# A hybrid encoder block: input projections and retention output by seven products for eight, with the token blocks kept in SBUF and the retention run head by head

## The chip, the cores and the metric

The kernel runs on one core of one Trainium2 chip. The time is the device time of one execution in microseconds (us); the three runs shown are summed up by their median. A core has TensorE (PE, with its weight loads PEld), VectorE (DVE), ScalarE (ACT), GpSimd (POOL) and a queue that issues the transfers (SP).

## The reference, cut to what matters

D_MODEL is 1024, the sequence 1024 tokens with 16 meta tokens ahead of it, all in float32. One projection of 5792 columns feeds two token mixers and their gates:

```python
def _mixer(u, w_in, ...):
    proj = u @ w_in
    rq, rk, rv, rg, a_cq, a_ckv, a_kr, a_gret, a_gmla = jnp.split(proj, SPLIT_IDX, axis=-1)
    rq = _apply_rope(rq ...); rk = _apply_rope(rk ...) * (RET_DK ** -0.5)      # 8 heads of 64
    y_ret = _head_group_norm(_bidir_retention(rq, rk, rv, decay_f, decay_b), gn_w)   # dv 128
    y_ret = (jax.nn.silu(rg) * y_ret) @ w_ret_out
    c_q, c_kv = _rmsnorm(a_cq, q_norm_w), _rmsnorm(a_ckv, kv_norm_w)           # ranks 384, 256
    ...                                                                        # MLA attention, 8 heads
    merged = jax.nn.sigmoid(a_gret) * y_ret + jax.nn.sigmoid(a_gmla) * y_mla
    return merged @ w_o
```

u is the RMS norm of x. The retention works in chunks of 128 tokens: inside a chunk scores times a decay mask, between chunks a state that is carried forward and one backward. After the mixer come a residual sum, a SwiGLU FFN with its own norm, and a final norm.

## The kernel before

A float32 product is made of three matmuls in the chip's fp32r type (`mm3`, L122 to L124): each operand is split into a high part (an ACT cast) and a low part (a DVE subtraction), and high by high, high by low and low by high are summed in PSUM.

*Input projections.* u is held transposed as eight pairs of tiles `uh`/`ul` of 128 by 1040. `weights()` (L112 to L118) loads 128 output columns and splits them; `gemm` walks eight k tiles, so each 512 columns of result take 24 matmuls. v is made the other way round, tokens as the output rows, with 256-column products; pair 0's v is made while x comes in (L236 to L238).

*Retention.* Four pairs of heads. For each pair v, the rotated q and k and two gates (rg, through Silu) are projected and stay in SBUF; then `core(p, ...)` runs both heads: k transposed and weighted (`kw`), chunk sums u (L376), a scan of 14 DVE steps (L379, L382), and for each half of four chunks scores (L388), the mask (L390), y (L394, L395), the group norm (L400 to L406), a transposition (L409) and the product with Silu (L411), whose result z goes to DRAM (`z_d`). A scheduler orders each engine's instructions by what is ready and by the order of the program, so projections of the next work stand between the pieces of a head.

*After it.* Six sigmoid gates of the attention branch go to `s_d`. z comes back in eight tiles, split by ACT (L456) and POOL (L457); then for each of eight column tiles a gate product (L437, L438) and the product with w_ret_out, whose sum is multiplied by the gate (L467) into `r_d`. Then the latents ckv and cq (L490, L491), their norms, the shared rotary key, the rotary queries, the last two gates, and the attention. The FFN already uses `seven`: of a product of 2 by 2 blocks (256 output columns, 512-token halves) it makes seven block products "11", "t2", "t3", "n1", "21", "t4", "22" from sums and differences of blocks, where eight would do without sums. They share four PSUM banks; POOL makes the weight sums, ACT and DVE split them (L925, L926), and DVE puts the four results together.

## Time and profile before

| what | value |
|---|---|
| median of three runs | 1809.23 us (1808.49 to 1812.77) |
| the profiled execution | 1811.09 us, its span 1809.3 us, granted TensorE clock 0.994 |
| busy in the span | PE 1776.5 us, DVE 1117.9, ACT 788.1, POOL 628.5 |
| matmuls of the plain input projections and retention output | L122 to L124: 496 + 128 of 512 columns each, and narrower ones |
| first matmul, first score of the attention | 4.95 us, 736.8 us |

Busy is the time in which an engine executed something. A row of windows reads: from:to, its length, then for PE, PEld, DVE, ACT and POOL the busy time with the count of instructions begun in it, the granted clock, the DMA share and GB/s. A group's row has line, engine, operation, output<-inputs, shape, count, then busy us and mean ns of one, then idle time before it and what ended it. A row of the timeline has start and duration in us, and in brackets the idle time before it.

### The profile page before, as it was taken

The numbers are of one execution on the slowest core, as the hardware profiler recorded it, in microseconds if no ns is written. First come the engines' busy times: TensorE is split into PE (matmuls) and PEld (weight loads), VectorE is DVE, ScalarE is ACT, GpSimd is POOL, SyncE is SP. The second block draws the span as 40 slices with busy tenths as digits, with TensorE's granted clock in tenths as the row PEclk, the third lists the DMA queues.
The fourth block names the chain that finished last, engine by engine and source line by source line (L and its number), as shares of the span: only waits on it lengthen the run. The fifth ranks groups of instructions, "written<-read, shape, count | busy, mean of one in ns | idle before, by whom it ended". The sixth has DMA issues, their size and how long they took to land.

```text
span 1809.3 us, 25989 instructions
## 1 busy us (share of the span) xinstructions
PE 1776.5 (98%) x9434; PEld 1525.2 (84%) x9434; DVE 1117.9 (62%) x2124; ACT 788.1 (44%) x1461; POOL 628.5 (35%) x523
## 2 busy tenths in 40 slices
PE   8999999999999999999999999999999999999997
PEld 8898989888788898899989888788888888777787
DVE  6655454544222253787879666876666666877866
ACT  6724242433211133677778445533333333544434
POOL 5303030301200012143242432676667666533422
PEclk9999999999999999999999999999999999999999
DMA  6011111114312212210112555333332333754512
GB/s 218 36 47 49 46 54 41 53 70 146 117 70 71 78 43 85 69 47 28 38 49 71 178 171 174 100 105 107 107 119 88 105 105 105 235 198 150 153 51 93
DMA packets 92495, 175.02 MB, mean 97 GB/s; under 512 B 12032, under 2 KB 26944, under 8 KB 92368
## 3 DMA queue, kind: packets, MB, share of 16 engines
q1 hardware_dynamic: 92368, 173.38, 28.9%
q8 instruction: 74, 1.21, 0.3%
q14 instruction: 53, 0.43, 0.1%
HBM read 129.58 MB, written 43.69 MB: 96 GB/s over the span
## 4 chain that ended last, share of the span: by engine, by line
PE 85%; DVE 6%; ACT 3%; DMA 2%; issue 2%; POOL 1%; SPq 0%; DVEq 0%; POOLq 0%; ACTq 0%
PE mm L934 28%; PE mm L122 13%; PE mm L123 13%; PE mm L124 13%; PE o L693 3%; PE t L663 2%; DVE slot L139 1%; PE s L122 1%; PE s L123 1%; PE s L124 1%; DMA slot<-f_d 1%; PE tr L388 1%; PE y L395 1%; PE u L376 1%; PE y L394 1%
## 5 line engine op out<-in xcount | busy, mean ns | idle before, releaser
L934 PE MATMUL mm<-slot,slot 128*128 128x512 f32 x2604 | 595.6, 390 | 8.4 <-DVE slot L926 3.8
L934 PEld LDWEIGHTS mm<-slot,slot 128*128 128x128 f32 x2604 | 489.1, 188 | 113.8 <-DVE slot L926 5.8
L925 ACT CAST slot<-slot 128x512 fp32r<-128x512 f32 (+1 forms) x238 | 138.7, 583 | 292.5 <-PE mm L934 285.4
L122 PE MATMUL mm<-uh,wh 128*128 128x512 f32 (+2 forms) x640 | 242.6, 379 | 1.0 <-DVE rk L331 0.6
L123 PE MATMUL mm<-ul,wh 128*128 128x512 f32 (+2 forms) x640 | 243.5, 380 | 0.0
L124 PE MATMUL mm<-uh,wl 128*128 128x512 f32 (+2 forms) x640 | 242.3, 379 | 0.0
L926 DVE TENSOR_TENSOR slot<-slot,slot 128x512 fp32r<-128x512 f32 (+1 forms) x238 | 200.5, 843 | 34.4 <-ACT slot L925 34.1
L122 PEld LDWEIGHTS mm<-uh,wh 128*128 128x128 f32 x640 | 120.3, 188 | 23.7 <-DVE rk L331 1.0
L124 PEld LDWEIGHTS mm<-uh,wl 128*128 128x128 f32 x640 | 120.5, 188 | 21.0
L123 PEld LDWEIGHTS mm<-ul,wh 128*128 128x128 f32 x640 | 120.1, 188 | 20.8
L117 ACT CAST wh<-wr 128x1024 fp32r<-128x1024 f32 x51 | 53.2, 1049 | 152.5 <-PE mm L123 120.6
L139 DVE TENSOR_TENSOR slot<-slot,slot 128x512 fp32r<-128x512 f32 x123 | 102.4, 847 | 15.2 <-ACT slot L138 14.9
L653 DVE TENSOR_SCALAR_CACHE_REDUCE pr<-s,sq_c 128x384 f32<-128x384 f32 (+1 forms) x192 | 103.2, 573 | 7.7 <-PE t L671 5.6
L138 ACT CAST slot<-slot 128x512 fp32r<-128x512 f32 x123 | 74.6, 620 | 71.3 <-DMA slot<-f_d 29.4
L124 PE MATMUL mm<-slot,slot 128*128 128x512 f32 (+1 forms) x288 | 105.4, 366 | 0.0
L123 PE MATMUL mm<-slot,slot 128*128 128x512 f32 (+1 forms) x288 | 105.3, 366 | 0.0
L122 PE MATMUL mm<-slot,slot 128*128 128x512 f32 (+1 forms) x288 | 105.2, 367 | 0.0
L666 DVE TENSOR_TENSOR ptl<-t,pth 128x512 fp32r<-128x512 f32 x128 | 85.7, 684 | 19.6 <-ACT pth L665 18.9
L665 ACT CAST pth<-t 128x512 fp32r<-128x512 f32 x128 | 71.9, 580 | 26.0 <-PE t L663 25.6
L910 POOL TENSOR_TENSOR slot<-slot,slot 128x512 f32<-128x512 f32 (+1 forms) x34 | 50.2, 1478 | 90.1 <-DVE slot L926 31.1
L118 DVE TENSOR_TENSOR wl<-wr,wh 128x1024 fp32r<-128x1024 f32 x51 | 67.5, 1326 | 19.1 <-ACT wh L117 17.4
L913 POOL TENSOR_TENSOR slot<-slot,slot 128x512 f32<-128x512 f32 (+1 forms) x34 | 43.2, 1272 | 103.4 <-DVE slot L926 99.9
(349 smaller groups left out, 3582.7 us busy)
## 6 DMA issues: line engine op xcount, KB each, us to landing
wr<-in_w_in SPq DMA_DIRECT2D x37, 512.0 KB
f_d<-slot SPq DMA_DIRECT2D x71, 256.0 KB
slot<-f_d SPq DMA_DIRECT2D x71, 256.0 KB
slot<-in_w_g SPq DMA_DIRECT2D x44, 256.0 KB
slot<-in_w_u SPq DMA_DIRECT2D x44, 256.0 KB
slot<-in_w_dq SPq DMA_DIRECT2D x48, 192.0 KB
slot<-in_w_o SPq DMA_DIRECT2D x32, 256.0 KB
z_d<-ay SPq DMA_DIRECT2D x16, 256.0 KB
```

The source lines that it names most:

```text
L118: dve.tensor_sub(lo, raw, f(hi))
L122: pe.matmul(ps, sh, mh, start=start, stop=False)
L123: pe.matmul(ps, sh, ml, start=False, stop=False)
L124: pe.matmul(ps, sl, mh, start=False, stop=stop)
L138: act.copy(hi, t)
L139: dve.tensor_sub(lo, t, f(hi))
L653: dve.tensor_scalar(pr[:, c], ps[:, :n], sq_c[:, qb : qb + 1], None, ALU.mult, ALU.max, accum_out=mx[:, j : j + 1])
L665: act.copy(pt[0][d], tp)
L666: dve.tensor_sub(pt[1][d], tp, f(pt[0])[d])
L925: act.copy(hi, side[b])
L926: dve.tensor_sub(low, side[b], f(hi))
L934: pe.matmul(ps, sw[:, ks], sx, start=begins and q == qs[0] and i == 0, stop=q == nq - 1 and i == 2, skip_group_check=True)
```

## The change

All input projections (23 groups of 256 columns, `win(0)` to `win(22)`, in the order rg, v, q, k, both gates, ckv, cq with kr) and the retention output (4 groups) use `seven`, which moves ahead of them and takes its pools as an argument. The 14 tiles by 4 of u's blocks (`U`, high and low of seven block forms) stay in SBUF until the latents are made; the same buffers then take z's blocks (`Z`). The 16 meta tokens have narrow matmuls of their own (L214). Results that were used at once now go to DRAM and come back: rg, v (transposed on TensorE first), q, k and both sets of gates.

```diff
+    def seven(pools, srcs, blocks, meta=None):
+        wr, ws, wh_, wl_, pm_ = pools
...
+        pool.tensor_add(s1, a21, a22)
+        pool.tensor_sub(s2, s1, a11)
+        pool.tensor_sub(a21, a11, a21)
+        side = {"11": a11, "t2": s2, "t3": a21, "n1": s1, "21": a12, "t4": a22, "22": s2}
...
+        def prod(b, qs=range(nq)):
...
+                if b == "22":
+                    pool.tensor_sub(s2, s2, a12)
...
+                act.copy(hi, side[b])
+                dve.tensor_sub(low, side[b], f(hi))
...
+                for i, (sw, sx) in enumerate(((wh, xh), (wh, xl), (wl, xh))):
+                    pe.matmul(ps, sw[:, ks], sx, start=begins and q == qs[0] and i == 0,
+                              stop=q == nq - 1 and i == 2, skip_group_check=True)
...
+    def seven_out(prod, pl, post, rest=None):
...
+        act.copy(e, prod("11", r[0]))
+        dve.tensor_add(e, prod("t2", r[1]), e)
...
-        pm = sb(c1, "ps_mm", 3, space=PSUM)
-        pc = sb(c1, "ps_core", 1, space=PSUM)
-        pt2 = sb(c1, "ps_turn", 2, space=PSUM)
+        bt1 = sb(c1, "tokens", 4)
+        wr1, ws1 = sb(c1, "w1r", 5), sb(c1, "w1s", 2)
+        wh1, wl1 = sb(c1, "w1h", 3), sb(c1, "w1l", 3)
+        cr = sb(c1, "c1", 6)
+        pm = sb(c1, "ps_mm", 5, space=PSUM)
+        pc = sb(c1, "ps_core", 3, space=PSUM)
...
+        def bsplit(nm, t):
+            hi, lo = mk(bt1, (P, 512), "h" + nm, F32R), mk(bt1, (P, 512), "l" + nm, F32R)
+            act.copy(hi, t)
+            dve.tensor_sub(lo, t, f(hi))
+            return hi, lo
...
+                U[q]["11"] = bscale("11", x11, w1)
+                act.mul(g12, x12, w1)
+                dve.scalar_tensor_tensor(n1, x11, w1, g12, ALU.mult, ALU.subtract)
+                act.mul(g22, x22, w2)
+                pool.tensor_add(t2, g22, n1)
+                U[q]["t2"] = bsplit("t2", t2)
...
+        cw = sb(cc, "core", 1)
+        ay = sb(cc, "ay", 6)
...
+        def z_sums(p):
+            n1, t3, t2, t4 = [slot(ay) for _ in range(4)]
+            for t, i in ((n1, 0), (t3, 7), (t2, 6), (t4, 4)):
+                load(t, z_d[p, i])
+            pool.tensor_sub(n1, n1, t3)
+            pool.tensor_sub(t3, t2, t3)
+            pool.tensor_add(t2, t2, n1)
+            pool.tensor_sub(t4, t4, t2)
+            for t, i in ((n1, 3), (t3, 2), (t2, 1), (t4, 5)):
+                store(z_d[p, i], t)
...
+        fillers = [(2, rg_post(2)), (3, rg_post(3))]
+        fillers += [(12 + i, gate_post(g_d if i < 4 else s_d, 2 * (i % 4))) for i in range(8)]
...
+        for p in range(4):
+            t = core_pair(p)
+            for h in range(2):
+                core(p, h, *t)
+                filler()
+            z_sums(p)
+        while fillers:
+            filler()
+        cc.close()
...
+        Z = [{} for _ in range(4)]
+        for i, nm in enumerate(NAMES):
+            for q in range(4):
+                raw = slot(cr)
+                load(raw, z_d[q, i])
+                Z[q][nm] = bsplit(nm, raw)
...
+        for j in range(4):
+            seven_out(seven(w7, A["w_ro"][j], Z), cr, ret_post(j))
```

Line numbers after: in `seven` the weight sums are L183 to L185 and L199, the weight split L201 and L202, the matmul L209, those of the meta tokens L214 (48 rows by 128); `seven_out` puts the quarters together in L225 to L234. Splits of blocks are L260 and L261; with the norm's weight L267, in the sums of the first part L308 and L325. `core`'s tiles q, k, v, `qw` and `st`, some of them in two buffers before, have one each. Its chunk sums are L535, scores L552, the mask L554, y L558 and L559, the norm L564 to L570, the transposition L573 and z L574; the sums of z are L581 to L587. The latents are L626 and L627, their squares' sums L634, z's loads L709, the rotary queries L717 to L746, the product with the gate L753. Where the code says that a filler follows each head, the scheduler may take its matmuls earlier, as each engine is free.

How the engines' rows stand at three places. First DVE at the program's start. Before, `ul` is a tile of u's low part, `wl` one of v's weights:

```order
L229 SCALAR_TENSOR_TENSOR ul_26_118<-xk_69_173,cols_74,uh_18_110 128x256
L231 TENSOR_TENSOR wl_164<-wr_162,wh_163 128x256
L229 SCALAR_TENSOR_TENSOR ul_26_118<-xk_69_173,cols_74,uh_18_110 128x272
L229 SCALAR_TENSOR_TENSOR ul_26_118<-xk_69_173,cols_74,uh_18_110 128x512
L229 SCALAR_TENSOR_TENSOR ul_27_119<-xk_70_174,cols_74,uh_19_111 128x1040
L231 TENSOR_TENSOR wl_164<-wr_162,wh_163 128x256
L229 SCALAR_TENSOR_TENSOR ul_28_120<-xk_71_175,cols_74,uh_20_112 128x1040
L231 TENSOR_TENSOR wl_164<-wr_162,wh_163 128x256
L229 SCALAR_TENSOR_TENSOR ul_29_121<-xk_72_176,cols_74,uh_21_113 128x1040
```

After, `l`, `lt`, `ln` are low parts of blocks "11", "t2" or "t3", and "n1"; slots are weights or sums of blocks:

```order
L267 SCALAR_TENSOR_TENSOR l_47_174<-slot_137,cols_74,h_46_173 128x512
L202 TENSOR_TENSOR slot_196<-slot_139,slot_195 128x512
L308 SCALAR_TENSOR_TENSOR slot_170<-slot_137,cols_74,slot_169 128x512
L202 TENSOR_TENSOR slot_212<-slot_148,slot_211 128x512
L202 TENSOR_TENSOR slot_204<-slot_156,slot_203 128x512
L261 TENSOR_TENSOR l_141_451<-slot_171,h_140_450 128x512
L261 TENSOR_TENSOR ln_53_191<-slot_170,hn_52_190 128x512
L267 SCALAR_TENSOR_TENSOR l_83_261<-slot_250,cols_74,h_82_260 128x512
L202 TENSOR_TENSOR slot_228<-slot_140,slot_227 128x512
L308 SCALAR_TENSOR_TENSOR slot_257<-slot_250,cols_74,slot_256 128x512
L261 TENSOR_TENSOR lt_49_182<-slot_172,ht_48_181 128x512
L267 SCALAR_TENSOR_TENSOR l_98_313<-slot_302,cols_74,h_97_312 128x512
```

Where two kinds alternated, block differences, block splits and weight splits now stand in one row, a 512-column piece each; they reach to row 62.

Second, TensorE at the end of the retention. Before, `mm` is a gate of the attention branch and `tr_3601` the last transposition of the last head:

```order
L122 MATMUL mm_3968<-uh_22_114,wh_3935 128x512
L123 MATMUL mm_3968<-ul_30_122,wh_3935 128x512
L124 MATMUL mm_3968<-uh_22_114,wl_3936 128x512
L122 MATMUL mm_3968<-uh_23_115,wh_3935 128x512
L409 MATMUL tr_3601<-ident_63,ay_3596 128x128
L123 MATMUL mm_3968<-ul_31_123,wh_3935 128x512
L409 MATMUL tr_3601<-ident_63,ay_3596 128x128 x2
L124 MATMUL mm_3968<-uh_23_115,wl_3936 128x512
L409 MATMUL tr_3601<-ident_63,ay_3596 128x128
L122 MATMUL mm_3968<-uh_24_116,wh_3935 128x512
L123 MATMUL mm_3968<-ul_32_124,wh_3935 128x512
L124 MATMUL mm_3968<-uh_24_116,wl_3936 128x512
```

After, `mm_4658` is y and `mm_4685` the transposition of head 7's second half, `mm_5391` the sums of the key norm, and `mm_5424` the second half of group 21 (the query latent):

```order
L559 MATMUL mm_4658<-st_4573,qw_4570 128x128
L558 MATMUL mm_4658<-v_4566,slot_4656 128x128
L559 MATMUL mm_4658<-st_4573,qw_4570 128x128
L573 MATMUL mm_4685<-ident_63,slot_4680 128x128
L677 MATMUL mm_5380<-ident_63,slot_5377 128x16
L573 MATMUL mm_4685<-ident_63,slot_4680 128x128 x3
L677 MATMUL mm_5380<-ident_63,slot_5377 128x16
L152 MATMUL mm_5391<-ones_68,lss_5188 128x1 x8
L152 MATMUL mm_5391<-ones_68,lss_5188 16x1
L209 MATMUL mm_5424<-h_124_414,slot_5499 128x512
L209 MATMUL mm_5424<-l_125_415,slot_5499 128x512
L209 MATMUL mm_5424<-h_124_414,slot_5500 128x512
```

The products that stood among the pieces of the last head now stand ahead of it and behind it; from row 2236 to 2285 there is no L209. POOL at that place, after, where `lss` holds the squares for the key norm and L582 to L585 are the sums of pair 3:

```order
L547 TENSOR_TENSOR slot_4647<-slot_4647,rstd_b_125 128x512
L634 TENSOR_TENSOR lss_5188<-lss_5188,slot_5374 128x512
L582 TENSOR_TENSOR slot_4844<-slot_4844,slot_4845 128x512
L583 TENSOR_TENSOR slot_4845<-slot_4846,slot_4845 128x512
L584 TENSOR_TENSOR slot_4846<-slot_4846,slot_4844 128x512
L585 TENSOR_TENSOR slot_4847<-slot_4847,slot_4846 128x512
L634 TENSOR_TENSOR lss_5188<-lss_5188,slot_5351 128x512
L634 TENSOR_TENSOR lss_5188<-lss_5188,slot_5388 128x16
L199 TENSOR_TENSOR slot_5574<-slot_5574,slot_5568 128x512
```

The squares' last sums, which L152 needs, have come to stand behind the sums of z.

Third, the retention output. Before, TensorE's first product with z (`zh`) stands between gate products:

```order
L122 MATMUL mm_4068<-uh_25_117,wh_4058 128x512
L123 MATMUL mm_4068<-ul_33_125,wh_4058 128x512
L124 MATMUL mm_4068<-uh_25_117,wl_4059 128x512
L122 MATMUL mm_4096<-zh_537_4010,wh_4064 128x512
L122 MATMUL mm_4123<-uh_18_110,wh_4058 128x512
L123 MATMUL mm_4123<-ul_26_118,wh_4058 128x512
L124 MATMUL mm_4123<-uh_18_110,wl_4059 128x512
L122 MATMUL mm_4123<-uh_19_111,wh_4058 128x512
```

After, DVE's row ahead of the weights of block "21" of the first output group (`slot_6189`); `l_1231` and `l_1234` are the last two of 28 subtractions that split z, `mm_6013` to `mm_6067` the rotary queries:

```order
L261 TENSOR_TENSOR l_1231_5960<-slot_5957,h_1230_5959 128x512
L261 TENSOR_TENSOR l_1234_5966<-slot_5963,h_1233_5965 128x512
L739 TENSOR_TENSOR slot_6033<-mm_6013,slot_6009 128x512
L740 TENSOR_TENSOR slot_6034<-mm_6023,slot_6010 128x512
L739 TENSOR_TENSOR slot_6043<-mm_6023,slot_6009 128x512
L740 TENSOR_TENSOR slot_6044<-mm_6013,slot_6010 128x512
L744 TENSOR_TENSOR slot_6033<-slot_6033,slot_6038 128x512
L744 TENSOR_TENSOR slot_6043<-slot_6043,slot_6048 128x512
L739 TENSOR_TENSOR slot_6077<-mm_6057,slot_6053 128x512
L740 TENSOR_TENSOR slot_6078<-mm_6067,slot_6054 128x512
L202 TENSOR_TENSOR slot_6189<-slot_6100,slot_6188 128x512
L739 TENSOR_TENSOR slot_6087<-mm_6067,slot_6053 128x512
```

The split of z moved from POOL to DVE, and the weights of the fifth product stand behind all of it and behind the rotary queries' first part; TensorE's row has 48 matmuls of that group ahead of this product.

More of the change, by code (lines that the diff above doesn't have):

```diff
@@ L19 @@
 NS, NT, NO = 3, 3, 2
-G2 = 6
 D = 1024
@@ L166, in build, with half @@
+    def half(name):
+        return slice(0, 512) if name[1] == "1" else slice(512, 1024)
     right, right2 = ExitStack(), ExitStack()
@@ new lines, in squares, with input_norm @@
+                    pool.tensor_add(ss[c], ss[c], t)
+        def input_norm():
+            t = slot(xl)[:, : KT * NM]
+            load(t, A["xm"])
+            act.square(t, t)
+            dve.tensor_reduce(ssm, t.rearrange("p (k t) -> p t k", t=NM), axis=AX.X, op=ALU.add)
+            ps = mk(pc, (P, 512), "mm")
+            for b in range(NB):
+                pe.matmul(ps[:, b : b + 1], ss[b // 4][:, (b % 4) * P : (b % 4) * P + P], ones, start=True, stop=True)
+            pe.matmul(ps[:NM, NB : NB + 1], ssm, ones, start=True, stop=True)
@@ new lines, in z_sums, with gate_post, post @@
+        def z_sums(p):
[8 more added lines that the diff above has]
+                store(z_d[p, i], t)
+        def gate_post(dst, m0):
+            def post(name, t):
+                cs = half(name)
+                g = slot(cr) if name == "11" else t
+                (dve if name == "11" else pool).tensor_mul(g, t, rstd_b[:, cs])
+                act.activation(g, g, AF.Sigmoid)
+                store(dst[m0 + int(name[0]) - 1, :, cs], g)
+            return post
@@ new lines, in build, with kv_post @@
+        tail = slice(S, L)
+        ps = mk(pm, (P, 512), "mm")
+        def kv_post(name, t):
+            k = int(name[0]) - 1
+            latent_part(t, half(name), *ckv[k], column(C_KVN + k), name in ("11", "22"))
+        seven_out(seven(w7, win(20), U, (ps, M1 | M2)), cr, kv_post)
+        t = meta_sum(ps, 0, 256)
+        pt = mk(pc, (P, 512), "mm")
+        for k in range(2):
+            pe.transpose(pt[:, k * NM : k * NM + NM], t[:, k * P : k * P + P], ident[:NM, :NM])
+            latent_part(pt[:, k * NM : k * NM + NM], tail, *ckv[k], column(C_KVN + k), k == 0)
@@ new lines, in build @@
+        swp = sb(right, "skv", 1, side="right")
+        skv_b = mk(swp, (P, L), "skv_b")
+        fill(swp, 112)
+        wa = sb(right, "wa", 1, side="right")
+        spread(pc, "mm", skv_b, skv_c, list(range(NB + 1)))
+        qr_d = [[mk(dram, (P, S), f"qr{i}{j}") for j in range(2)] for i in range(2)]
+        wx = []
+        for i in range(2):
+            raw = slot(wr1)[:, :384]
+            load(raw, A["w_uq"][4 + i])
+            hi, low = slot(wh1, F32R)[:, :384], slot(wl1, F32R)[:, :384]
+            act.copy(hi, raw)
+            dve.tensor_sub(low, raw, f(hi))
+            wx.append((hi, low))
@@ new lines, in build @@
+        for lo, n in RCH:
+            c = slice(lo, lo + n)
+            cm, sm = slot(cr), slot(cr)
+            load(cm, A["cM"][:, c])
+            load(sm, A["sM"][:, c])
+            xx = []
+            for i in range(2):
+                ps = mk(pm, (P, 512), "mm")
+                gemm(ps, wx[i], cq, 3, lo, n)
+                xx.append(ps)
+            for i in range(2):
+                ta, tb_ = slot(cr), slot(cr)
+                dve.tensor_mul(ta, xx[i], cm)
+                dve.tensor_mul(tb_, xx[1 - i], sm)
+                (pool.tensor_add if i else pool.tensor_sub)(ta, ta, tb_)
+                hi = slot(cr, F32R)
+                act.copy(hi, ta)
+                dve.tensor_sub(ta, ta, f(hi))
+                store(qr_d[i][0][:, c], f(hi))
+                store(qr_d[i][1][:, c], ta)
@@ L588, in build, with ret_post, post @@
+        def ret_post(j):
+            def post(name, t):
+                m, cs = 2 * j + int(name[0]) - 1, half(name)
+                g = slot(cr)
+                load(g, g_d[m, :, cs])
+                dve.tensor_mul(g, t, g)
+                store(r_d[m, :, cs], g)
+            return post
+        for j in range(4):
+            seven_out(seven(w7, A["w_ro"][j], Z), cr, ret_post(j))
     with ExitStack() as c1:
+        qk = sb(c1, "qk", 3)
         vp = sb(c1, "v", 1)
```

831 lines of the change are left out of this document (395 added, 436 removed).

## The prediction

> **What bounds the kernel now.** I read the page's busy shares and chain first, then TensorE's groups by shape, then windows of single stages, then the timeline of one head of the retention. From the page:
>
> ```profile
> PE 1776.5 (98%) x9434; PEld 1525.2 (84%) x9434; DVE 1117.9 (62%) x2124; ACT 788.1 (44%) x1461; POOL 628.5 (35%) x523
> PE 85%; DVE 6%; ACT 3%; DMA 2%; issue 2%; POOL 1%; SPq 0%; DVEq 0%; POOLq 0%; ACTq 0%
> GB/s 218 36 47 49 46 54 41 53 70 146 117 70 71 78 43 85 69 47 28 38 49 71 178 171 174 100 105 107 107 119 88 105 105 105 235 198 150 153 51 93
> ```
>
> TensorE is busy for 1776.5 of 1809.3 us and carries 85% of the chain that ended last. So a product that goes is time that goes, as long as TensorE is still fed. The pace is the distance between starts, not the mean of one (matmuls overlap); windows with nothing but 512-column matmuls give it, and two rows each of the timeline give the narrow ones:
>
> ```profile
> 0.00:50.00 50.00, 42.93 (x287) 40.01 (x288) 31.46 (x37) 34.22 (x52) 24.48 (x34) 0.97 0.55 197
> 500.00:550.00 50.00, 50.00 (x219) 40.81 (x219) 11.13 (x13) 6.54 (x8) 0.00 (x0) 1.00 0.19 68
> 1250.00:1300.00 50.00, 50.00 (x222) 41.44 (x221) 31.45 (x41) 16.01 (x27) 32.35 (x22) 1.00 0.31 104
> 269.79 0.28 PE L122 MATMUL mm<-wh,uh 128*128 128x256 f32 x1
> 272.15 0.28 PE L124 MATMUL mm<-wh,ul 128*128 128x256 f32 x1
> 649.91 0.34 PE L523 MATMUL mm<-uh,wh 128*112 128x384 f32 x1
> 652.17 0.34 PE L523 MATMUL mm<-ul,wh 128*112 128x384 f32 x1
> ```
>
> 50/219 and 50/222 make 0.228 and 0.225, so 0.227 us for 512 columns. Twenty steps of 256 columns lie between 269.79 and 272.15 (0.118), thirteen of 384 between 649.91 and 652.17 (0.174). In 500 to 550, the gate and output products of before, DVE works 11 us of 50 and POOL none: that cover is large. In 1250 to 1300, where the FFN already runs seven products for eight, DVE works 31 and POOL 32.
>
> **The change on TensorE.** The groups that go (L122, L123 and L124 are thirds of one product, so each stands for three):
>
> ```profile
> L122 PE MATMUL mm<-uh,wh 128*128 128x512 f32 x496 | 196.1, 395 | 1.0 <-DVE rk L331 0.6 <-DVE sw L341 0.4
> L122 PE MATMUL mm<-wh,uh 128*128 128x256 f32 x192 | 54.9, 286 | 0.0
> L122 PE MATMUL mm<-zh,wh 128*128 128x512 f32 x128 | 49.4, 391 | 0.3 <-DVE g L467 0.3
> L122 PE MATMUL mm<-uh,wh 128*128 128x384 f32 x96 | 32.8, 342 | 0.0
> L122 PE MATMUL mm<-uh,wh 128*128 128x272 f32 x48 | 13.8, 287 | 0.0
> ```
>
> 512 columns: 3 x (496 + 128) = 1872 x 0.227 = 425. 384: 288 x 0.174 = 50. 272: 144 x 0.125 (0.118 scaled by columns) = 18. 256: 3 x 192, and 192 more of the first loop (L236 to L238), 768 x 0.118 = 91. The shared key's 48 (L523) and the 64 of the meta tokens (L315) add 15. Gone: 599 us. Added: 27 groups of 256 output columns, each 7 products x 4 x 3 = 84 matmuls of 512, so 2268 x 0.227 = 515; 240 narrow matmuls for the meta tokens (L214) at about 0.08, between 0.06 and 0.11, 19; 64 transposes of v, 7. Together 541. **TensorE does 58 us less.** What is asked is how much of this comes back as waits.
>
> **Prices of the other engines**, all from before:
>
> ```profile
> L926 DVE TENSOR_TENSOR slot<-slot,slot 128x512 fp32r<-128x512 f32 x154 | 147.4, 957 | 33.6 <-ACT slot L925 33.3 <-issue 0.2
> 1269.43 1.70 DVE L926 TENSOR_TENSOR slot<-slot,slot 128x512 fp32r<-128x512 f32 x1 [1.26 <-ACT slot L925]
> 1274.07 0.68 DVE L926 TENSOR_TENSOR slot<-slot,slot 128x512 fp32r<-128x512 f32 x1
> L876 DVE SCALAR_TENSOR_TENSOR slot<-slot,cols,slot 128x512 fp32r<-128x512 f32 x8 | 6.0, 751 | 1.5 <-ACT slot L875 1.5
> L437 DVE TENSOR_TENSOR g<-mm,rstd_b 128x512 f32<-128x512 f32 x32 | 22.1, 691 | 86.9 <-PE mm L124 86.4 <-DMA r_d<-g 0.3
> L891 DVE SCALAR_TENSOR_TENSOR slot<-slot,cols,slot 128x512 f32<-128x512 f32 x4 | 4.9, 1231 | 0.0
> L913 POOL TENSOR_TENSOR slot<-slot,slot 128x512 f32<-128x512 f32 x22 | 28.9, 1312 | 54.3 <-DVE slot L926 53.6 <-POOL slot L972 0.7
> ```
>
> A split's subtraction takes 0.68 when DVE has the way free, up to 1.70 while POOL works, 0.96 in the mean. [...]
>
> **Start, +10 (5 to 16).** Before's window 0 to 50 holds 287 matmuls: 256 of 256 columns (30 us at its pace) and 31 mostly of 512 (7), so 37 us of work by 50, some 13 behind. After, the first 168 matmuls (38 us) need nearly all blocks of u: on DVE 16 scalings (0.75 to 1.23, take 0.9), 38 subtractions (0.68 to 0.96, take 0.85) and 8 sums from PSUM (0.69) stand in its first 62 rows, 14 + 32 + 6 = 52 us. With the 5 us before the first data these end at 57 to 60; TensorE is then 20 to 23 behind instead of 13.
>
> **v and the rotated keys, +4 (0 to 10).** 192 us of products; DVE, ACT and POOL are each about 80% full in the rotation. No row shows that mixture; 1250 to 1300 above (63%, 32%, 65%, nothing lost) is nearest and says near nothing, so I take the low side of the middle.
>
> **Heads with a product behind each, +8 (0 to 30).** Ten products are dealt out, one after each head. A head with its product is 40 us of TensorE against some 30 of DVE and 28 of POOL. The core's buffers are now single, so head h+1 loads v after head h's last use of it. That chain is some 15 to 25 us, shorter than 40.
>
> **The last head and a half with nothing behind it, +31 (25 to 45).** By the order shown above, TensorE's rows 2236 to 2285 hold the end of head 6, all of head 7 and the sums for the key norm, and no product; the next one stands behind them. Cause: the latent tiles take over the core's memory, so their writes queue on DVE and ACT behind the last head, and L152 waits for POOL, which first makes the sums of pair 3 from z that went out and came back. What a half head costs in series, before:
>
> ```profile
> 433.27 0.38 PE L394 MATMUL y<-v,ay 128*128 128x128 f32 x2
> 435.25 0.89 DVE L400 BATCH_NORM_STATS2 bn<-y 128x6 f32<-128x128 f32 x4 [2.02 <-PE y L395]
> 436.45 0.30 ACT L402 ACTIVATE sd<-mv,gneps 128x4 f32<-128x4 f32 x1 [2.59 <-DVE mv L401]
> 437.00 1.37 DVE L406 TENSOR_SCALAR ay<-y,mv,sd 128x128 f32<-128x128 f32 x4
> L382 DVE SCALAR_TENSOR_TENSOR st<-st,gch,u 64x128 f32<-64x128 f32 x56 | 19.8, 354 | 11.0 <-PE u L376 9.0
> SPq L686 <- DMA l_d<-rr: 21.8, 26, 2.0
> ```
>
> From y's start at 433.27 to the end of the normalised tile at 438.37 are 5.1 us, four times 20.4. Twice the next scores and their mask, 2 x 2.1; the transposes and z, 1.2 + 1.5; head 7's u 1.8; its scan of 14 steps, at 0.35 and some 0.02 between, 5.2; a mask 0.7; z out and in again at up to 2.0 each, 4; four POOL sums at 1.31, then the norm's 1.8; L152 0.9. Sum 46.7. TensorE has 15.4 us of work in it, so 31 are lost; where four waits overlap better 25, with half the clock and slower loads 45. Before, the same half heads lie between gate products and cost nothing.
>
> **Transfers, 0 (0 to 6).** rg, v, q and k (4.2 MB each) and pair sums of z now go out and come back, some 37 MB more in about 550 us, 67 GB/s on top of slices of 36 to 70; the page's slices reach 235 GB/s. They stand on SP's queue ahead of later weight loads, which are issued a product early; that product's 19 us is the cover, and without it each would cost a load of about 2 us.
>
> **z's blocks, +20 (13 to 32).** After the rotary products TensorE does the small sums, 48 matmuls of the first output product (10.9 us) and then waits for the block "21", whose weights are split on DVE behind all 28 z subtractions and eight more operations. The z splits begin only when the last norm is through, since they stand behind it on ACT and DVE, and their loads on SP behind the last store of the shared key: 3 + 2.2 for the norm and a table load, 0.6 for the first cast, 28 x 0.75 = 21, 8 x 0.69 = 5.5, 0.85: 33, less 12.7 of TensorE work. 28 x 0.68 and an overlap give 13, 28 x 0.96 with slow loads 32 (7.3 MB come in; the page's best slice moves 235 GB/s, which is 31 us, and 412 GB/s, the row below, 18). Before, POOL split z beside gate products.
>
> ```profile
> 12.00:14.00 2.00, 0.46 (x2) 0.46 (x3) 2.00 (x2) 2.00 (x3) 2.00 (x3) 0.83 1.05 412
> 692.00:694.00 2.00, 2.00 (x11) 1.97 (x12) 0.05 (x1) 0.17 (x1) 0.10 (x1) 0.64 0.00 0
> 694.00:696.00 2.00, 2.00 (x7) 2.00 (x8) 1.51 (x5) 1.12 (x3) 0.20 (x1) 0.50 0.50 130
> 696.00:698.00 2.00, 2.00 (x9) 2.00 (x8) 0.00 (x0) 0.00 (x0) 0.00 (x0) 0.50 0.35 132
> ```
>
> **Gone with the old order, -5 (-15 to 0):** the stretch of granted clock 0.64, 0.50, 0.50 from 692 to 698 and the wait ahead of it, 5 us; other short waits of the old projections may go too. The three further output products (57 us) and the way into attention I take as unchanged; the FFN is.
>
> **Sum:** -58 + 10 + 4 + 8 + 31 + 20 - 5 = +10 on the profiled execution's own 1811.1, so 1821. The median of the runs lies 1.9 under that execution: 1819.
>
> **The rivals.**
> *The splits run free (faster).* If DVE meets POOL seldom, a split costs 0.68 and not 0.85 in the start, in the heads and for z: 38 x 0.17 = 6 and 28 x 0.07 = 2, the head stage 8 less, the rotation 4 less, and with DVE early the two bare stretches fall to their lower ends, 6 and 5 less: 31 off, 1788. It decides from a mean of about 0.75 on for the subtractions of L202 and L261. For it: the 0.68 row. Against: POOL sums stand among them all through.
> *It cancels.* The bare stretches at 25 and 15 with all else as taken: 11 off, 1808.
> *DVE bounds the heads.* At 1.0 per split and with single buffers the head stage loses 30, not 8: 1841. For it: the L926 mean; against: DVE at 63% in 1250 to 1300 without loss.
> *Half the clock through the bare stretch.* The clock rows above show 0.50 after a wait. In the bare stretch TensorE's 12 us that lie in the chain would take 24: 1831. [...]
>
> **How the numbers follow.** Forecast 0.30; free splits 0.29; cancel 0.20; half clock 0.12; DVE-bound heads 0.09. A measurement of this kernel tells apart about 0.3%, 5.4 us. The free splits and the low tail of the cancelling case are faster, 0.33; the rest of that case and the low end of the forecast are the same, 0.19; the others slower, 0.48. Range 1784 to 1848: from the free splits with a few us more to the DVE-bound heads with a few more; the forecast's own is 1808 to 1832.
>
> **What would show it.** TensorE busy 50 to 60 us less. DVE over 95% busy in the first 57 us. No L209 row for some 45 us around the last head, with L152 behind POOL at its end. A wait of 15 to 25 us between the 48th and 49th matmul of the first output product, released by DVE L202. Wrong if either bare stretch is under 12 us lost, or if the heads lose over 25.

## The result and the profile after

The changed kernel takes 1873.19 us (median of 4 runs, 1871.53 to 1875.22), before 1811.0 in runs beside it (4 runs, 1808.49 to 1813.02): a ratio of 1.0345, 95% interval [1.0325, 1.0365]. That is slower, as forecast, but by 62 us where 8 to 10 were named, and above the upper end of the range. The profiled execution of the changed kernel took 1871.53 with a span of 1869.8. Its page, where the first rows are busy time, the next ones 40 slices of 46.7 us, and the last one the chain that ended last:

```profile
PE 1746.0 (93%) x8821; PEld 1461.1 (78%) x8821; DVE 1337.9 (72%) x2391; ACT 902.5 (48%) x1649; POOL 859.9 (46%) x680
PE   5799999999995749999999999999999999999998
PEclk8899999999997869999999999999999999999999
PE 78%; DVE 10%; DMA 5%; issue 3%; ACT 2%; POOL 1%; SPq 0%; DVEq 0%; POOLq 0%; ACTq 0%
```

TensorE is busy 30.5 us less than before, and the span is 60.5 longer, so its idle time grew by 91 us. Two places in its row show it: the first two slices, and slices 13 to 15, 561 to 701 us. All else but the last slice reads 9. DVE's share of the chain went from 6 to 10%, DMA's from 2 to 5%.

Busy time flatters the holes, since a matmul lasts longer at half clock: from 671.97 to 675.80, at a granted clock of 0.50, those of 512 columns start 0.43 us apart and not 0.227. So I count each matmul by the median distance between the starts of two neighbours of its shape, both traces taken together (0.227 us for 512 columns, 0.110 for 128x128, 0.060 for the meta tokens' L214), and call the rest of a stretch lost. The work is then 1666.5 us against 1730.9, and lost are 203.3 against 78.4:

| stretch of the span, us | lost before | lost after | difference | forecast (sum's terms) |
|---|---|---|---|---|
| 0 to 100 | 13.9 | 49.0 | +35 | +10 |
| 100 to 550 | 17.3 | 21.3 | +4 | +12 |
| 550 to 750 | 6.4 | 83.5 | +77 | +46 (31 + 20 - 5) |
| 750 to the end | 40.8 | 49.5 | +9 | 0 |
| TensorE's work | | | -64 | -58 |
| sum | | | +60.5 | +10 |

The windows show the same stretches, two of the kernel before and then those of the changed kernel (columns: busy time and instructions of PE, PEld, DVE, ACT, POOL, then the granted clock, the DMA share and GB/s):

```profile
550.00:650.00 100.00, 100.00 (x492) 86.75 (x491) 25.56 (x32) 20.93 (x32) 4.10 (x6) 1.00 0.22 72
650.00:750.00 100.00, 99.33 (x475) 85.00 (x474) 53.82 (x108) 41.48 (x70) 18.00 (x18) 0.97 0.24 79
```

```profile
0.00:50.00 50.00, 26.52 (x72) 17.47 (x72) 41.88 (x46) 27.95 (x48) 24.36 (x28) 0.90 0.40 133
100.00:550.00 450.00, 446.98 (x2335) 365.51 (x2333) 303.57 (x567) 233.22 (x372) 241.85 (x164) 1.00 0.38 129
565.00:602.00 37.00, 23.39 (x109) 19.51 (x107) 20.39 (x73) 11.99 (x16) 12.27 (x9) 0.71 0.21 70
602.00:618.00 16.00, 0.70 (x3) 0.59 (x4) 3.35 (x7) 3.90 (x10) 5.17 (x5) 0.50 0.31 115
672.00:701.00 29.00, 5.08 (x14) 3.61 (x13) 23.22 (x33) 17.24 (x30) 4.21 (x3) 0.56 0.80 264
```

**End of the heads.** Between 602 and 618 no engine is busy for even 6 of 16 us; what is under way is a chain of transfers. The timeline there, first TensorE, then ACT, then POOL (behind each row the idle time before it and what ended it):

```profile
600.11 0.30 PE L573 MATMUL mm<-ident,slot 128*128 128x128 f32 x1 [2.34 <-DVE slot L570]
616.83 0.28 PE L677 MATMUL mm<-ident,slot 16*128 16x16 f32 x1 [15.37 <-ACT lss L629]
617.59 3.57 PE L152 MATMUL mm<-ones,lss 128*128 128x1 f32 x16 [0.48 <-POOL lss L634]
```

```profile
612.92 0.72 ACT L626 ACTIVATE ckh<-slot,cols 128x512 fp32r<-128x512 f32 x1 [13.61 <-DMA z_d<-slot]
```

```profile
599.18 1.26 POOL L582 TENSOR_TENSOR slot<-slot,slot 128x512 f32<-128x512 f32 x1 [2.94 <-DMA slot<-z_d]
606.87 1.26 POOL L583 TENSOR_TENSOR slot<-slot,slot 128x512 f32<-128x512 f32 x1 [6.43 <-DMA slot<-z_d]
609.55 1.26 POOL L585 TENSOR_TENSOR slot<-slot,slot 128x512 f32<-128x512 f32 x1
```

The chain that ended last has these transfers there, and ACT's tiles behind them (start, duration):

```profile
602.27 2.01 DMA z_d<-slot
604.36 2.35 DMA slot<-z_d
610.84 1.99 DMA z_d<-slot
613.55 2.05 ACT ckh L626 x4
```

The last head's z went out, the last pair's z came back for its sums, POOL summed until 610.8, the sums went out again, and only then could ACT write the first latent tile (L626), because that tile takes the memory from which z's sums were being stored. ACT's 13.61 us of waiting end with that store, and so do TensorE's 15.37 us, once the latents are written, squared and summed.

**z's blocks.** TensorE's row, and the groups of DVE between 670 and 701 (busy time and mean ns):

```profile
700.37 0.76 PE L209 MATMUL mm<-ht,slot 128*128 128x512 f32 x1 [23.92 <-DVE slot L739]
```

```profile
L261 DVE TENSOR_TENSOR lt<-slot,ht 128x512 fp32r<-128x512 f32 x12 | 10.0, 865 | 1.0 <-ACT ht L260 1.0
L261 DVE TENSOR_TENSOR l<-slot,h 128x512 fp32r<-128x512 f32 x12 | 8.2, 692 | 5.1 <-ACT h L260 4.8
L261 DVE TENSOR_TENSOR ln<-slot,hn 128x512 fp32r<-128x512 f32 x4 | 2.7, 686 | 0.3 <-ACT hn L260 0.2
```

The 28 splits take 21 us of work, and 28.6 from the start of the first to the end of the last (669.81 to 698.43), most of the rest being waits for ACT, which itself waits for z's loads at 264 GB/s. The releaser is L739 (a read of the rotary products, which stands in DVE's row behind the 28 splits and gives a PSUM bank back), not the weights of "21" as forecast, and the wait comes after 12 matmuls of the output product and not after 48.

### The profile page after: what moved, and what is told of

It reads as the page before. It is cut to its first block, busy times and chain, and to the rows that moved or that the text cites. A ratio compares the mean times of both kernels' runs of the same rounds, so it can differ in the third digit from the quotient of the medians.

```text
span 1869.8 us, 26307 instructions
## 1 busy us (share of the span) xinstructions
PE 1746.0 (93%) x8821; PEld 1461.1 (78%) x8821; DVE 1337.9 (72%) x2391; ACT 902.5 (48%) x1649; POOL 859.9 (46%) x680
## 4 chain that ended last, share of the span: by engine, by line
PE 78%; DVE 10%; DMA 5%; issue 3%; ACT 2%; POOL 1%; SPq 0%; DVEq 0%; POOLq 0%; ACTq 0%
PE mm L209 51%; PE mm L129 3%; PE mm L130 3%; PE mm L131 3%; PE o L866 3%; PE t L836 2%; DVE slot L146 2%; PE s L129 1%; DVE slot L202 1%; PE s L130 1%; PE s L131 1%; DMA slot<-z_d 1%; DMA slot<-f_d 1%; DMA slot<-in_xT 1%; PE mm L552 1%
## 5 line engine op out<-in xcount | busy, mean ns | idle before, releaser
L209 PE MATMUL mm<-slot,slot 128*128 128x512 f32 x2604 | 597.2, 391 | 10.9 <-DVE slot L202 5.4
L209 PEld LDWEIGHTS mm<-slot,slot 128*128 128x128 f32 x2604 | 489.9, 189 | 117.1 <-DVE slot L202 7.8
L201 ACT CAST slot<-slot 128x512 fp32r<-128x512 f32 (+1 forms) x427 | 254.7, 599 | 471.3 <-PE mm L209 393.2
L202 DVE TENSOR_TENSOR slot<-slot,slot 128x512 fp32r<-128x512 f32 (+1 forms) x427 | 391.7, 919 | 97.8 <-ACT slot L201 89.5
L209 PE MATMUL mm<-ht,slot 128*128 128x512 f32 x648 | 224.5, 407 | 28.9 <-DVE slot L739 23.9
L209 PE MATMUL mm<-h,slot 128*128 128x512 f32 x648 | 228.1, 410 | 18.3 <-ACT slot L201 12.4
L209 PEld LDWEIGHTS mm<-ht,slot 128*128 128x128 f32 x648 | 124.7, 194 | 56.2 <-issue 28.2
L199 POOL TENSOR_TENSOR slot<-slot,slot 128x512 f32<-128x512 f32 (+1 forms) x61 | 83.3, 1365 | 178.3 <-DVE slot L202 144.8
L183 POOL TENSOR_TENSOR slot<-slot,slot 128x512 f32<-128x512 f32 (+1 forms) x61 | 84.8, 1391 | 174.0 <-DVE slot L202 50.2
L209 PEld LDWEIGHTS mm<-h,slot 128*128 128x128 f32 x648 | 125.6, 195 | 46.8 <-ACT slot L201 13.5
L209 PE MATMUL mm<-l,slot 128*128 128x512 f32 x324 | 130.8, 404 | 1.3 <-DVE l L267 1.3
L209 PE MATMUL mm<-lt,slot 128*128 128x512 f32 x324 | 129.8, 401 | 0.1
L146 DVE TENSOR_TENSOR slot<-slot,slot 128x512 fp32r<-128x512 f32 x123 | 107.4, 889 | 14.5 <-ACT slot L145 14.1
L184 POOL TENSOR_TENSOR slot<-slot,slot 128x512 f32<-128x512 f32 (+1 forms) x61 | 80.7, 1323 | 63.2 <-DVE slot L202 61.1
L129 PE MATMUL mm<-slot,slot 128*128 128x512 f32 (+1 forms) x288 | 105.2, 367 | 0.0
L185 POOL TENSOR_TENSOR slot<-slot,slot 128x512 f32<-128x512 f32 (+1 forms) x61 | 87.7, 1437 | 1.8
L838 ACT CAST pth<-t 128x512 fp32r<-128x512 f32 x128 | 71.6, 579 | 24.0 <-PE t L836 23.6
```

The lines of the kernel that those rows point to most:

```text
L129: pe.matmul(ps, sh, mh, start=start, stop=False)
L146: dve.tensor_sub(lo, t, f(hi))
L183: pool.tensor_add(s1, a21, a22)
L185: pool.tensor_sub(a21, a11, a21)
L199: pool.tensor_sub(s2, s2, a12)
L201: act.copy(hi, side[b])
```

## The experiments

Each kernel below is the change but for its edit; ratios are to the kernel before, in runs beside it. An edit shifts the line numbers behind it by a few (L209 of the change is L211 in some, and the plain eight products have L129 to L133).

Theory at the start: from the last head on, the work forms one chain (core, z out and in, latents, norms, rotary queries, z in and split, output) whose parts take over each other's memory, with no product left to lie beside it; and at the start, DVE's splits hold back what TensorE can do. The rivals said that each hole has a local cause (a place in a row, a bank, one engine) and closes when that is removed.

### The retention output by eight products again

z then needs 16 split tiles and no sums (`z_sums` goes); TensorE gets 48 matmuls, 10.9 us, more.

```diff
-            z_sums(p)
-        for i, nm in enumerate(NAMES):
+        for i, nm in ((0, "11"), (4, "21"), (7, "t2"), (6, "22")):
...
-            seven_out(seven(w7, A["w_ro"][j], Z), cr, ret_post(j))
+            for m, (a, b) in enumerate(((0, 3), (1, 2))):
...
+                        for q in range(4):
+                            mm3(ps, wh[:, ks], wl[:, ks], *Z[q][nm], k + q == 0, k == 1 and q == 3)
```

> The retention output alone goes back to eight products: z is split as 16 half tiles instead of 28 blocks, the block sums of z (POOL, and their way through DRAM) are gone, TensorE does 48 matmuls of 512 more (+11 us). Theory (bare stretches): the loads and splits of z, 28 us with TensorE waiting, shrink to about 16 (-12), and the latents' memory is free when z of head 7 is stored, about 8 us sooner than now, so the bare end of the heads loses 8 less; sum -9, about 1864 us. Rival (the rotary queries and norms set that stretch, not z): only the +11 shows, with a few us off the heads' end, 1878 to 1884.

Measured 1855.42, ratio 1.0231 [1.0212, 1.0249]: 18 us faster than the change, with 10.9 us more for TensorE. That is more than either side expected. By the count of the table, 7.6 us less are lost from 550 to 650, as expected, and 20.9 less from 650 to 750, where 12 were expected. TensorE's row:

```profile
607.77 0.28 PE L665 MATMUL mm<-ident,slot 16*128 16x16 f32 x1 [6.92 <-ACT lss L617]
676.45 0.77 PE L129 MATMUL mm<-ht,slot 128*128 128x512 f32 x1 [8.17 <-DVE slot L727]
```

The 15.37 us became 6.92 and the 23.92 became 8.17. So z's round trip for its sums was about half of that one wait, but only a sixth of all that is lost at the end of the heads. The 12 tiles more, and what goes with them in the order of the products, were about half of what is lost from 650 to 750; this run doesn't part the two.

### Rotary queries ahead of z

z's loads and splits are written behind the rotary queries, so that DVE gives the banks back before it splits z.

```diff
-        Z = [{} for _ in range(4)]
-        for i, nm in enumerate(NAMES):
...
         qr_d = [[mk(dram, (P, S), f"qr{i}{j}") for j in range(2)] for i in range(2)]
...
+        Z = [{} for _ in range(4)]
+        for i, nm in enumerate(NAMES):
```

> Only the code of the rotary queries moves ahead of z's loads and splits, so that DVE reads their four PSUM banks before it splits z. Theory (the second block product of the first output group waits 24 us for a bank that the rotary queries hold): the wait behind its 12th matmul goes, 48 matmuls run while z is split, and a shorter wait stands ahead of the 49th; 5 to 8 us less, 1865 to 1868. Rival (the split of z is the chain, the bank only where it shows): the same wait stands ahead of the 49th matmul and the rotary reads push the split of z back: 1871 to 1876.

Measured 1874.46, 1.0345 [1.033, 1.0361]: nothing gained, as the rival said. The wait moved:

```profile
688.22 0.80 PE L209 MATMUL mm<-h,slot 128*128 128x512 f32 x1 [17.41 <-ACT h L260]
713.73 0.80 PE L209 MATMUL mm<-h,slot 128*128 128x512 f32 x1 [7.18 <-ACT slot L225]
```

The 23.92 us are now 17.41 + 7.18. The bank was where the wait showed, and z's loading and splitting what it cost.

### Latent products as cover for the last heads

The latent products leave the chain: they are made behind heads 6 and 7 from the blocks still at hand, go out to memory (`lt_d`), and the latents are loaded from there.

```diff
+    lt_d = mk(dram, (6, P, S), "lt_d")
...
+        def lat_post(k):
+            def post(name, t):
+                store(lt_d[k + int(name[0]) - 1, :, half(name)], side_copy(name, t))
+            return post
...
+        while fillers:
+            filler()
+        latents()
         cc.close()
```

> The latent products (groups 20 to 22) write to DRAM like the gates and are read back when the core's memory is free, so that they are ready as cover for heads 6 and 7; nothing else moves. Theory (the last heads lose because no product is left to lay beside them): the waits between 565 and 621 us, 46 us, fall to 10 to 15, and splitting the latents after the heads, ACT 13 and DVE 8 us with TensorE idle, gives 10 to 15 back: 1845 to 1855. Rival (the heads' chain sets the end whatever lies beside it and the latents' chain only moves behind it): 1868 to 1878.

Measured 1870.36, 1.0314 [1.0299, 1.033]: 3 us less than the change by the medians, 6 by the ratios, whose intervals overlap. The window up to 600 is covered now, and next to nothing is won, as the rival said (windows, and TensorE's waits):

```profile
565.00:600.00 35.00, 35.00 (x189) 28.40 (x188) 25.65 (x60) 14.30 (x23) 13.09 (x9) 1.00 0.44 141
```

```profile
631.13 0.28 PE L699 MATMUL mm<-ident,slot 16*128 16x16 f32 x1 [11.30 <-ACT lss L647]
658.69 0.19 PE L710 MATMUL mm<-ident,slot 16*48 16x16 f32 x1 [13.50 <-DMA slot<-lm_d]
697.22 0.77 PE L211 MATMUL mm<-ht,slot 128*128 128x512 f32 x1 [23.52 <-DVE slot L752]
```

The transposition of the shared key's metadata, the second of these rows, waits 13.50 us where it waited 3.31 in the change: as I read it, the products that used to run there had covered the norms, but its releaser is now the load of these rows from memory, which the change doesn't have, and no run parts the two. The first row is the change's wait of 15.37 us, now 11.30. So the loss of the last heads came back behind them.

### Cover, with z split early and eight products

On top of the last one, z of the first three pairs is loaded and split behind the heads, and the output is made by eight products.

```diff
+        def zsplit(qs):
+            for i, nm in ((0, "11"), (4, "21"), (7, "t2"), (6, "22")):
+                for q in qs:
...
+        zsplit(range(3))
         cc.close()
```

> Three edits together: the latent products through DRAM as cover, the retention output by eight products, and z's tiles of pairs 0 to 2 loaded and split ahead of the latents. Theory (bare stretches, each with its own cause): the gains of the two first add, about -35, and with 12 of 16 z tiles split while the last heads run another 8 to 12 go: 1825 to 1835. Rival (one chain behind all three): no better than the better of the two single edits, 1845 or more.

Measured 1850.72, 1.0209 [1.0192, 1.0226], which is 4.7 below eight products alone, with intervals that overlap. Waits of 6.61, 5.22, 11.13 and 5.32 us remain in TensorE's row, at two of the last heads' transpositions, the metadata of the shared key and the first output product. The rival for this run (one chain behind all three edits, so that the gains don't add) was right.

### Latents and rotary queries behind output groups

What then is left to lie beside the latents is the output itself. z is early, as above (seven products kept); the last pair's z and output group 0 come first, then latents and norms, groups 1 and 2, the rotary queries (with the core's PSUM banks), group 3.

```diff
+        zsplit((3,))
+        for j in range(0, 1):
+            seven_out(seven(w7, A["w_ro"][j], Z), cr, ret_post(j))
         halves = (slice(0, 512), slice(512, 1024))
...
+        for j in range(1, 3):
...
         qr_d = [[mk(dram, (P, S), f"qr{i}{j}") for j in range(2)] for i in range(2)]
...
+        for j in range(3, 4):
```

> As cover (latent products through DRAM), with z's blocks of pairs 0 to 2 split ahead, and the latents' and the rotary queries' work behind the first and third of the four output groups, rotary products in the core's PSUM banks. All seven products stay. Theory (one chain of core, latents, rotary queries and z with TensorE idle beside it; only what stands behind it in the program can cover it): the output products, 76 us, now cover the latents, and of the 86 us lost between 565 and 712 some 20 to 35 stay: 1815 to 1830. Rival (contention of DVE, ACT and transfers: the same work takes its time wherever it stands): as cover, 1860 to 1872.

Measured 1852.05, 1.0224 [1.0207, 1.0242]: 21 us gained, under half of what the theory expected (43 to 58). The rival (the same work takes its time wherever it stands, 1860 to 1872) was wrong too. One wait of 24 us stayed, from 668 on, at the transposition of the shared key's metadata, which stands in TensorE's row with the sums of the second norm ahead of the remaining output groups:

```profile
692.25 0.19 PE L732 MATMUL mm<-ident,slot 16*48 16x16 f32 x1 [23.61 <-DMA slot<-lm_d]
```

### The start: POOL's block sums on DVE

```diff
-                pool.tensor_add(t2, g22, n1)
+                dve.tensor_add(t2, g22, n1)
-                pool.tensor_sub(g12, g22, g12)
+                dve.tensor_sub(g12, g22, g12)
```

> In the first 40 us the eight block sums of POOL (L310, L312) are DVE's. Theory (POOL slows DVE there): of the 13 DVE pieces of about 1.75 us before 40 us at most 6 stay, each of the others falls to 0.68 to 0.75; 8 pieces of 0.68 come in, and DVE's row 46 ends 3 to 8 us sooner; the time 1865 to 1871. Rival (the start loses because half of its products stand behind the first results, whatever DVE's speed): the pieces get shorter but the time stays at 1871 to 1875.

Measured 1871.01, 1.0317 [1.0302, 1.0332]: 2 us faster by the medians and 5 by the ratios, whose intervals overlap; that is where theory and rival meet. Two of DVE's groups in the first 36 us, the change first, then this kernel:

```profile
L202 DVE TENSOR_TENSOR slot<-slot,slot 128x512 fp32r<-128x512 f32 x5 | 6.5, 1307 | 0.3 <-ACT slot L201 0.3
L325 DVE SCALAR_TENSOR_TENSOR slot<-slot,cols,slot 128x512 f32<-128x512 f32 x2 | 3.6, 1776 | 0.0
```

```profile
L202 DVE TENSOR_TENSOR slot<-slot,slot 128x512 fp32r<-128x512 f32 x6 | 4.0, 681 | 0.0
L325 DVE SCALAR_TENSOR_TENSOR slot<-slot,cols,slot 128x512 f32<-128x512 f32 x2 | 1.5, 740 | 0.0
```

In these two groups the price per operation halves, as the free-splits rival wanted; over all of DVE's operations in that window the mean falls from 1.24 us (24 of them) to 0.82 (38), some splits still taking 1.4. But DVE has the eight sums more, and what TensorE had done by 50 us rises only from 16.3 to 18.8 us. A slow split is not the start's main loss.

### The start: the first two groups by eight products

All eight results of the two groups stand in eight banks at once and are fed block by block as u arrives; 24 matmuls, 5.4 us, more. With this the blocks come in another order, and the sums of weights and of quarters go for these groups.

```diff
+            def feed(q, k, g, xs):
...
+                        for i, (sw, sx) in enumerate(((wh, xh), (wh, xl), (wl, xh))):
+                            pe.matmul(bank[j, m, g], sw[:, ks], sx, start=q + k + i == 0, ...)
...
+                U[q]["11"] = bscale("11", x11, w1)
+                feed(q, 0, 0, U[q]["11"])
```

> Only the first two groups (rg 0 and 1, made as x comes in) are plain eight products: each scaled and split half of u feeds 12 matmuls at once instead of 6; 24 matmuls more (+5.4 us), one more split of x for each of four quarters. Theory (the start lacks matmuls for each DVE piece): TensorE is through some 75 to 85 us of paced work at 100 us instead of 52, the time falls by 18 to 25, 1848 to 1855. Rival (what bounds the start is DVE's total of block splits or the transfers, which stay): under 8 us, 1865 or more.

Measured 1864.55, 1.0292 [1.0275, 1.0309]: 8.6 us gained net, under half of what the theory expected (18 to 25) and at the edge of the rival (under 8). TensorE has 71.6 us of work done by 100, where 75 to 85 were expected and the change has 51.0. The windows of this kernel, against 72 matmuls in the change's first 50 us:

```profile
0.00:50.00 50.00, 39.33 (x146) 30.71 (x147) 42.20 (x48) 29.78 (x50) 20.96 (x24) 0.97 0.45 153
50.00:100.00 50.00, 43.32 (x208) 34.50 (x207) 15.17 (x26) 23.37 (x50) 26.11 (x19) 0.93 0.60 193
```

DVE does as much in the first 50 us (42.20 us of 48 operations) as in the change (41.88 of 46), and TensorE gets 146 matmuls instead of 72. So the amount of DVE's work alone doesn't set the start; what its row is for does: four of the seven products (t2, t3, n1, t4) need sums over blocks before they can start, and the later products follow the first ones' results, whose reads (L226 to L228) stand behind splits. The run doesn't tell how much each of the two is worth. In DVE's row of the change:

```profile
47.25 0.68 DVE L202 TENSOR_TENSOR slot<-slot,slot 128x512 fp32r<-128x512 f32 x1
47.85 0.68 DVE L226 TENSOR_TENSOR slot<-mm,slot 128x512 f32<-128x512 f32 x1
48.46 1.37 DVE L261 TENSOR_TENSOR lt<-slot,ht 128x512 fp32r<-128x512 f32 x1
49.75 0.68 DVE L227 TENSOR_TENSOR slot<-mm,slot 128x512 f32<-128x512 f32 x1
```

and TensorE, waiting for that, starts the next product at 50.58, "2.99 <-DVE slot L227" in its row.

### Both ends together

The output groups interleaved as above, with eight products for the output, eight for the first two groups, and the metadata rows `xm` in memory of their own, loaded first (L214 had waited 6.85 us for them, until 87.41).

```diff
-        xm = slot(cr)[:, : KT * NM].rearrange("p (k t) -> p k t", t=NM)
+        xm = mk(rt, (P, KT * NM), "xm").rearrange("p (k t) -> p k t", t=NM)
```

> All of these together: tail7's order, the output by eight products from 16 half tiles, the start by eight products, and the meta tokens' tile out of the shared buffers (L214 waits 7 us at 80 us for it). If the causes are separate: 1873 - 45 (tail) - 20 (start) - 7 (meta) and between -8 and +8 for the eight products of the output: 1793 to 1809, below the kernel before at 1811. If one bound lies behind several of them: 1820 or more.

Measured 1806.78 (10 runs), 0.9978 [0.9968, 0.9988]. Its largest wait:

```profile
655.90 0.19 PE L764 MATMUL mm<-ident,slot 16*48 16x16 f32 x1 [14.84 <-DMA slot<-lm_d]
```

So in the next kernel the shared key and the second norm move behind the second output group; beside it run the same with seven products for the output, and the same with the first two groups by seven products as in the change (the metadata rows stay in memory of their own).

```diff
+        for j in range(1, 2):
...
         for c in halves:
             shared_key(lat_load(5, c)[:48], c)
...
-        for j in range(1, 3):
+        for j in range(2, 3):
```

> The best kernel so far (1806.8 us: output by eight products, latents by way of memory and normed behind the first output group, first two groups by eight products, the metadata rows in memory of their own) still waits 14.84 us at 641 in TensorE's row, at the transposition of the shared key's metadata and the sums behind it. Here the shared key's part and the second norm stand behind the second output group (96 products, 21.8 us), nothing else is changed. If that wait is only a place in TensorE's row: 1791 to 1797. If it shows a chain of loads and VectorE work that any place would meet: it appears again ahead of the rotary queries, 1803 to 1809.

> The same with the retention output by seven products, as the change has it (84 products a group for 96, 28 z tiles for 16, and z_sums in the loop over the heads). If the eight products only helped because the z tiles' chain stood open in TensorE's row, then with that chain behind other work the seven products give their 48 x 0.227 = 10.9 us: 1781 to 1788. If the 28 tiles' loading and splitting (28 x 0.7 us on VectorE, 228 to 350 GB/s) can't be hidden even here: 1800 to 1815, with a wait ahead of the first output group's second half.

> The first kernel of this call without the two first groups by eight products (they are made by seven, as in the change). If the start's loss goes to the end of the kernel in full, as the stage measured it (14 to 16 us at 100 us): 1806 to 1813, or 14 to 16 above the first of this call. If a part of it is taken up by later waits, as the start's change alone showed (8.6 us): 8 to 10 above it.

| kernel | us, median | ratio to before, 95% interval |
|---|---|---|
| shared key behind the second group | 1796.40 (1792.13 to 1800.81) | 0.9918 [0.99, 0.9936] |
| the same, output by seven products | 1828.91 (1826.66 to 1830.11) | 1.0098 [1.0082, 1.0115] |
| the same, first two groups by seven products | 1814.97 (1812.93 to 1821.0) | 1.0025 [1.0012, 1.0037] |

The first has 10 us less than its predecessor, as the theory of the place in TensorE's row expected, and beats both kernels: 0.8% below before. Its last waits there:

```profile
645.81 0.50 PE L131 MATMUL mm<-ht,slot 128*128 128x512 f32 x1 [2.29 <-DVE slot L724]
664.41 0.17 PE L781 MATMUL mm<-ident,slot 16*48 16x16 f32 x1 [1.98 <-DMA slot<-lm_d]
```

The second is a miss on both sides: with seven products for the output the kernel takes 32.5 us more than with eight, at 1829, where the expectations went from 1781 to 1815. Its waits of over 2 us at output products:

```profile
600.44 0.80 PE L211 MATMUL mm<-h,slot 128*128 128x512 f32 x1 [2.57 <-ACT h L262]
613.92 0.80 PE L211 MATMUL mm<-ht,slot 128*128 128x512 f32 x1 [6.50 <-ACT ht L262]
653.38 0.80 PE L211 MATMUL mm<-h,slot 128*128 128x512 f32 x1 [9.91 <-ACT slot L227]
690.32 0.80 PE L211 MATMUL mm<-h,slot 128*128 128x512 f32 x1 [4.87 <-ACT slot L227]
```

The first two wait for z's splits (L262), the other two for ACT's copies of finished products (L227): seven-product groups wait at both their ends, for more blocks in front and for quarters put together behind. Beside these, the shared key's metadata wait 6.20 us here, against 1.98 with eight products.

The third says that the start's edit is worth 18.6 us when the end is closed, a little more than the 14 to 16 expected, and 8.6 when it isn't. In the latter case, by the count of the table on its profiled execution (1868.45, the slowest of four), the kernel is 15 us ahead of the change at 100 us; 6 are lost again up to 550 and 5.5 behind 750, and the cause of that stays open.

## Why the prediction was wrong

**TensorE's work, -58.** By the count above it was -64: most of the difference is L214, at 0.060 us and not 0.08.

**Start, +10 (5 to 16): mis-sized, +35.** This is the term furthest outside its own range. DVE wasn't 95% busy, but 41.88 of 50 us; it had 52 operations behind it by 58 us, where 62 were forecast by 57 to 60. That near miss doesn't make the difference. The step that failed is "TensorE is then 20 to 23 behind instead of 13", which takes TensorE to run all of the first 168 products as their blocks come. It had 16.3 us of work done by 50, the 168th matmul started at 76.38, and 49.0 us were lost by 100: the products that depend on earlier results came later. The run with eight products in the first two groups (DVE as busy by 50, twice the matmuls) bears this out. 6.85 us more went to L214, which waited for the metadata rows, a load that stands behind a block buffer; the sum had no term for that.

**v, rotated keys and heads, +12: near the low end, +4.** From 100 to 550 the changed kernel loses 21.3 us against 17.3, though DVE works 303.57 of 450 us there. One product of 19 us behind each head covers it.

**Transfers, 0:** held from 100 to 550 (129 GB/s in that window). The term looked for loads late for a product; what mattered were stores late for the next tile in the same memory, and that belongs to the next term.

**End of the heads, +31 (25 to 45), and z, +20 (13 to 32): right mechanism, right places, both at the upper end.** With the -5 they make +46, measured +77 (44.9 and 38.5 lost, in the hundreds from 550 and from 650, less 6.4 that before lost in both). The first term's upper end was named for half the clock and slower loads, and both came. From 565 to 618 TensorE is idle for 28.9 us, near the 31 of the sum; its other 24.1 us hold 12.4 us of work at full pace, so the clock made up to 11.7 of the loss. The transfers of z take 6.4 us where 4 were taken, because the sum had no term for the last of them, the store that ACT waits for. Without z's sums 7.6 us less are lost there. In z's stretch the wait of 23.92 us lies within the 15 to 25 that were named, and the splits' 28.6 us are what the sum has for them and the operations behind them, 28. What failed is "less 12.7 of TensorE work": only 12 of the 48 matmuls had a bank to go to, 2.7 us of cover for 10.9, and the releaser was L739, not L202. The run with the rotary queries ahead shows that the bank itself wasn't the price. L152 did stand behind POOL at its end (617.59), and no L209 stood in TensorE's row from 565 to 618, as said.

**The range.** It took the upper ends one at a time, as rivals. They came together: with 16, 45 and 32 the same sum gives 1851, already above 1848. The signs of being wrong (a bare stretch under 12, heads over 25) didn't occur; of the signs of being right, TensorE's busy time fell by 30.5 us and not by 50 to 60, since slow matmuls count for longer (one of 512 columns 0.63 us at 671.97, at a granted clock of 0.50, and 0.39 at 559.79, at 1.00).

**The rivals.** The free splits fell: their condition, a mean of about 0.75 us, was not met (0.93 for the 215 subtractions of L202 and L261 with 512 columns up to 712 us; 692 and 686 ns for 16 of the 28 in z's stretch, which didn't close for that). "It cancels" fell with both bare stretches. Half the clock did occur: 0.71 and 0.50 in the rows above. From 565 to 712 TensorE's busy time is 90.6 us for 65.5 us of work at full pace, so up to 25 of the 82 us lost there are slow running and not waits. For the one hole that this rival priced, its 12 us are what came; it doesn't reach 62. DVE as the bound of the heads fell.

**A term that the sum lacked:** the +9 behind 750. It is spread in small pieces, and I have not traced it.

**DVE beside POOL.** In the first 36 us two of DVE's groups took 1307 and 1776 ns with POOL's block sums beside them, 681 and 740 ns without. The time hardly followed (1873.19 us with, 1871.01 without), since DVE's speed was not what mainly held the start.

## What to carry to other kernels

A saving in products is worth nothing at the places where the saving's own preparation is the chain: seven products for eight paid in the middle, where other products lay beside the block sums (by the count, +4 lost; no run has eight products there with the rest as it is), and cost 18 to 32 us in the retention output, where 12 more tiles of z and their sums had to be ready first, and 9 to 19 at the program's start. Count for each place what must be ready before the first matmul and what must be read before the next bank, and look in the order for what else TensorE has in its row meanwhile. When a hole is filled with work from elsewhere, check what that work covered there.

## What the runs showed of the hardware

The granted clock fell after some waits of about 2 us and not after another. In the changed kernel TensorE waited 2.31 us until 567.48 and 2.35 until 575.61; behind the first, the clock was 1.00 until 569.6 and then 0.56, behind the second 0.76. In the best kernel, a wait of 2.29 until 645.81 left it at 1.00, and one of 1.98 until 664.41 was followed by 0.50. The windows, of the change first and then of the best kernel:

```profile
569.60:573.00 3.40, 3.27 (x16) 3.25 (x16) 0.73 (x2) 0.35 (x1) 0.00 (x0) 0.56 0.21 80
575.60:578.00 2.40, 2.39 (x12) 1.89 (x13) 0.82 (x3) 1.54 (x2) 2.33 (x2) 0.76 0.26 100
```

```profile
645.80:648.00 2.20, 2.19 (x10) 1.81 (x11) 0.69 (x1) 0.00 (x0) 0.00 (x0) 1.00 0.97 318
666.00:668.00 2.00, 2.00 (x11) 2.00 (x11) 0.34 (x3) 0.00 (x0) 0.00 (x0) 0.50 0.25 67
```

What stands around the waits differs: 512-column matmuls on both sides of the one until 645.81, narrow ones behind the others. Where a wait lies in time differs too: in the changed kernel's record the clock switches at 570.03, 573.44, 576.86, 580.27 and 583.68, steps of 3.41 us (windows of 0.4 us from 570.0, 573.4, 576.8, 580.2 and 583.6 read 0.54, 0.95, 0.57, 0.92 and 0.60). The wait until 575.61 lies over one of these switches, the one until 567.48 over none. Which of these differences decides, no run here tested.
